# A hybrid decoder layer on one core: the down projection with VectorE and ScalarE in a hand-written issue order

## The chip, the core and the metric

The kernel runs on one core of a Trainium2 chip. The metric is the device time of one execution in microseconds (us). A step below is one product of one pair of feature chunks: 12 matmuls on TensorE (PE in the profile). VectorE is DVE there, ScalarE is ACT, GpSimd is POOL and SyncE is SP.

## What is computed

One layer over 1024 tokens of width 1024, all in float32: three mixers (pooling, sliding-window attention, spatial gating), then a gated convolution feed-forward network, whose second half is what the change is about:

```python
h = rms_norm(x, norm2[l])
up = causal_dwconv(h @ w_up[l], conv_w[l], conv_b[l])
gate, val = jnp.split(up, 2, axis=-1)
x = x + (jax.nn.silu(gate) * val) @ w_down[l]
```

The last line is the down stage. It contracts over 2816 features (22 chunks of 128) and adds its result to `out`, which holds the residual already.

## The kernel before, in words

Every float32 product is made from three matmuls: an operand is split into `hi` (ScalarE, line 86, a rounding copy) and `lo` (VectorE, line 87, the operand less `hi`), and hi·hi, hi·lo and lo·hi are added up in PSUM.

**The down stage** (from line 981) is one round of Strassen's method in Winograd's form. The 22 chunks make 11 pairs `q`; a pair's tile `raws[q]` has eight 128x512 blocks, A11 to A22 of the activations (`gd`, spilled to DRAM by the up stage) and B11 to B22 of `w_down`. From them come seven products, P1 to P7, and each product is accumulated in four PSUM banks over the pairs of a part. There are two parts, pairs 0 to 5 and 6 to 10, so 7 x 11 = 77 steps. `ORDERS` says in which order the products come: P1, P2, P6, P7, P4, P3, P5 in the first part, P5 ahead of P3 in the second. P1 and P2 share four banks, P6, P7 and P4 share four, P3 and P5 share four; a product that continues in banks of another one needs the other one read out first.

- `operands` makes the operands of one step: for P7 and P4 first a subtraction on VectorE (lines 1024 and 1029), then `split`. It is called three steps ahead (`ahead = 3`). `hi` has four buffers ("w") and `lo` has four ("x"), so the operands of step j+3 get theirs only when TensorE is done with step j-1.
- `presum` makes two sums for a pair (lines 1009 and 1010, VectorE), which P6, P5 and P4 use. It is called in the steps of P2.
- `evacuate` reads a product's banks after its last step: with ScalarE for P1 (line 1052) and P2 (line 1055), with VectorE for P6 and P7 (line 1058), P4 (line 1060), P3 (line 1064), P5 (line 1050) and the last result (line 1076). Results go to `out` by accumulating DMAs that POOL issues (`add`, line 1041). In the second part `olds` reads one quarter of `out` into SBUF, VectorE adds to it, and SP writes it with a plain DMA (line 1077).
- `fetch` loads a part's blocks with DMAs on SP (line 997): the halves for P1 and P2 of all pairs, then the other halves. The second part's `fetch` stands behind the first step of P3; its tiles use the buffers of the first part's (two "hh", five "hq", one of the five being the tile `sv` that keeps P1).
- `gate` (lines 879 to 885) is the last work of the up stage on a chunk: two convolutions (a ScalarE activation, line 871, and two VectorE operations, line 875, each), a Silu (line 883), a product (line 884) and the spill to `gd`. `conv` takes its output tile from the four "x" buffers too. At the end of the up stage the generators that are left run out, the last of them (chunk 21) behind `fetch`.

The program's text doesn't set the order on an engine: the framework's planner orders the instructions of each engine by a simulated timeline, so in the kernel before VectorE takes, for example, subtractions of P7 and P4 long before their steps. The four "raw" tiles of P2 (`raw`, three buffers) go out by DMA before a buffer is taken again.

Of the kernel before, what the change touches and what calls it, by code (L numbers as in the profile page):

```python
# [38 lines left out]
def trunk_kernel(tc, x, positions, norm1, w_in, q_norm, k_norm, sinks, w_pool, pool_scale,  # L39
                 sgu_v_norm, w_s, b_s, w_proj_a, w_proj_b, w_proj_c, w_out, norm2,  # L40
                 w_up, conv_w, conv_b, w_down, cst_d, out, dbg=None, stop=None):
    nc = tc.nc
    act, dve, pe, pool, sp = nc.scalar, nc.vector, nc.tensor, nc.gpsimd, nc.sync
    x, out = x[0], out[0]
# [34 lines left out]
    def sm2(n=T, dt=F32):  # L79
        return slot("sm2", 5, [P, n], dt)  # L80
# [35 lines left out]
    for dst, src in ((0, norm1), (8, norm2), (16, pool_scale)):  # L116
        n = src.shape[1] // P
# [92 lines left out]
    def new_h():  # L210
        return [t[:, k] for t in [slot("hh", 2, [P, HK, 2, T], F32R) for _ in range(2)] for k in range(HK)]
# [7 lines left out]
    h = new_h()  # L219
# [423 lines left out]
    st = Stream(w_in, 768, 256, KD, normed.ins)  # L643
    for t in range(2):
        kv = t4([P, NT, 256])
        qs = [t4([P, 2, T]) for _ in range(2)]
        st = tok_major(h, st, lambda i, ps: act.activation(kv[:, i, :], ps, AF.Copy), (w_in, 256, T, KD))
# [4 lines left out]
        st = tok_major(h, st, lambda i, ps: act.activation(qs[i // 2][:, i % 2, :], ps, AF.Copy), (w_in, 1024, T, KD))  # L652
# [9 lines left out]
        u, v = t4([P, NT, 256]), t4([P, NT, 256])  # L662
# [13 lines left out]
        part = slot("part", 1, [P, KD, T], F32)  # L676
# [34 lines left out]
        for i, c0 in enumerate(units):  # L711
            if i + 1 < len(units):
                wn = w_gran(w_in, units[i + 1])
            else:
                x2t = [slot("x2" if t == 0 else "x", 4, [P, D], F32) for _ in range(NT)]
                for b in range(NT):
                    r = t * T + b * P
                    sp.dma_start(x2t[b], x[r : r + P, :])
                st = Stream(w_out, 0, T, KD)
            if i >= 2:  # L720
                kind, n = ((i - 2) % 2, (i - 2) // 2) if i < 18 else (2, i - 18)
# [10 lines left out]
            ps = mm_ps()  # L732
# [15 lines left out]
        if t == 0:  # L748
            h = new_h()
# [6 lines left out]
        for nh in range(2):  # L756
# [6 lines left out]
            ahead = (w_out, T, T, KD) if nh == 0 else (w_in, 768, 256, KD) if t == 0 else None  # L763
            st = tok_major(merged, st, evo, ahead)
# [122 lines left out]
    gates = []  # L887
# [58 lines left out]
    while full:  # L946
        late = [(rest[0], n, REST) for n in REST] if rest and len(full) <= 2 * len(rest) else []
# [36 lines left out]
    raws, sums, ops = {}, {}, {}  # L984

    def two(r, a, b):
        return r[:, a : b + 1 : b - a, :]
# [11 lines left out]
    def fetch(a, b):  # L999
        for j, q in enumerate(range(a, b)):  # L1000
            raws[q] = slot("hh", 2, [P, 8, T], F32) if j in (0, 2) else h_([P, 8, T])
            sums[q] = {}
            load(q, (A11, B11, A12, B21))
        for q in range(a, b):
            load(q, (A21, B12, A22, B22))

    def presum(r, st):
        st["1"], st["2"] = q_([P, 2, T]), q_([P, 2, T])
        dve.tensor_tensor(st["1"], two(r, A21, B12), two(r, A22, B11), ALU.add)
        dve.tensor_tensor(st["2"], st["1"], two(r, A11, B22), ALU.subtract)  # L1010

    def operands(p, r, st):

        if p == "P1":
            src = two(r, A11, B11)
        elif p == "P6":
            src = st["2"]
        elif p == "P2":  # L1020
            src = two(r, A12, B21)
        elif p == "P7":
            src = two(r, A11, B12)
            dve.tensor_tensor(src, src, two(r, A21, B22), ALU.subtract)
        elif p == "P5":
            src = st["1"]
        elif p == "P4":
            d4 = two(r, A12, B21)
            dve.tensor_tensor(d4, d4, st["2"], ALU.subtract)
            src = two(r, A22, B21)  # L1030
        else:
            src = two(r, A12, B22)
# [4 lines left out]
    state = {}  # L1037

    def add(i, dh, o):

        pool.dma_start(out[i * P : (i + 1) * P, dh * T : (dh + 1) * T], o, accum_op=ALU.add)

    def evacuate(part, p, i, ps):


        if p == "P1" and i == 0:
            state["sv"] = h_([P, 8, T])
            state["v3"] = [sm2() for _ in range(NT)]
        s, v2, v3 = state["sv"][:, i, :], state["sv"][:, NT + i, :], state["v3"][i]
        over = lambda v: dve.scalar_tensor_tensor(v, v, -1.0, ps, ALU.mult, ALU.add)  # L1050
        if p == "P1":
            act.activation(s, ps, AF.Copy)
        elif p == "P2":
            o = raw([P, T])
            act.activation(o, ps, AF.Copy)
            add(i, 0, o)
        elif p in ("P6", "P7"):
            dve.tensor_tensor(v2 if p == "P6" else v3, s, ps, ALU.add)
        elif p == "P4":
            dve.tensor_tensor(s, s, ps, ALU.add)  # L1060
            add(NT + i, 0, s)
        elif part + 1 < len(parts):
            if p == "P3":
                dve.tensor_tensor(v3, v3, ps, ALU.add)  # L1064
            else:
                for ti, v in ((i, v2), (NT + i, v3)):
                    over(v)
                    add(ti, 1, v)
        elif p == "P5":
            over(v3)  # L1070
            add(NT + i, 1, v3)
            o = state["o"][:, i, :]
            dve.tensor_tensor(o, o, v2, ALU.subtract)
        else:
            o = state["o"][:, i, :]
            dve.tensor_tensor(o, o, ps, ALU.add)
            sp.dma_start(out[i * P : (i + 1) * P, T:], o)

    def olds():

        state["o"] = h_([P, NT, T])
        for i in range(NT):
            sp.dma_start(state["o"][:, i, :], out[i * P : (i + 1) * P, T:])

    todo = [(part, p, q) for part, (a, b) in enumerate(parts) for p in ORDERS[part] for q in range(a, b)]
    ahead = 3
    for g in gates[:-1]:
        for _ in g:
            pass
    fetch(*parts[0])  # L1090
    for g in gates[-1:]:
        for _ in g:
            pass
    for j in range(ahead):
        _, p, q = todo[j]
        ops[todo[j]] = operands(p, raws[q], sums[q])
    sets = {}
    for j, (part, p, q) in enumerate(todo):
        a, b = parts[part]
        start = q == a and p in ("P1", "P6", ORDERS[part][-2])  # L1100
        if start:
            sets[p] = [bank() for _ in range(NT)]
        ps = sets["P1" if p in ("P1", "P2") else "P6" if p in ("P6", "P7", "P4") else ORDERS[part][-2]]
        if p == "P2":
            presum(raws[q], sums[q])
        if p == "P4" and q == a and part + 1 == len(parts):
            olds()
# [63 lines left out]
```

## Time and profile before

| what | us |
|---|---|
| median of 3 runs (1332.35 to 1333.76) | 1332.39 |
| the profiled execution, its own time | 1330.77 |
| its span, from the first to the last instruction | 1329.0 |
| TensorE busy | 1290.5 (97%) |
| VectorE busy | 968.4 (73%) |
| ScalarE busy | 603.7 (45%) |

The span is cut from the hardware profiler's record of one execution. 1.77 us of that execution lie outside the span. Busy TensorE includes the run of a matmul through the array, so that 0.39 us of busy time stand for a new matmul every 0.227 us; lost time is therefore read from the starts of matmuls, not from the busy share.

### The profile page before, as it was taken

The numbers are of one execution on the slowest core, as the hardware profiler recorded it, in microseconds if no ns is written. First come the engines' busy times: TensorE is split into PE (matmuls) and PEld (weight loads), VectorE is DVE, ScalarE is ACT, GpSimd is POOL, SyncE is SP. The second block draws the span as 40 slices with busy tenths as digits, with TensorE's granted clock in tenths as the row PEclk, the third lists the DMA queues.
The fourth block names the chain that finished last, engine by engine and source line by source line (L and its number), as shares of the span: only waits on it lengthen the run. The fifth ranks groups of instructions, "written<-read, shape, count | busy, mean of one in ns | idle before, by whom it ended". The sixth has DMA issues, their size and how long they took to land.

```text
span 1329.0 us, 16065 instructions
## 1 busy us (share of the span) xinstructions
PE 1290.5 (97%) x5956; PEld 1065.6 (80%) x5956; DVE 968.4 (73%) x1516; ACT 603.7 (45%) x982; POOL 192.1 (14%) x123
## 2 busy tenths in 40 slices
PE   6999999999999999999999999999999998999998
PEld 6888888888888888888877877878878776787787
DVE  6887865544579676456575899889989979757865
ACT  5655554333465554333573434434444443433432
POOL 0000000000000000000005444444244400100302
PEclk9999999999999999999999999999999998999999
DMA  6422224322432222543554323323333174236705
GB/s 232 123 83 62 80 80 150 112 72 95 155 107 64 80 79 79 155 120 113 200 176 132 111 73 111 102 80 111 111 96 111 64 250 177 32 113 236 117 11 95
DMA packets 167644, 151.25 MB, mean 114 GB/s; under 512 B 7615, under 2 KB 132493, under 8 KB 167565
## 3 DMA queue, kind: packets, MB, share of 16 engines
q1 hardware_dynamic: 163533, 142.87, 33.8%
q0 software_dynamic: 4032, 7.34, 3.8%
q8 instruction: 47, 0.77, 0.2%
q14 instruction: 32, 0.26, 0.1%
HBM read 120.30 MB, written 29.88 MB: 113 GB/s over the span
## 4 chain that ended last, share of the span: by engine, by line
issue 53%; DVE 17%; PE 15%; DMA 6%; ACT 4%; POOL 1%; SPq 0%; DVEq 0%; ACTq 0%; POOLq 0%
DVE x L875 6%; PE bk L1115 4%; PE bk L1116 4%; PE bk L1114 4%; DMA raw<-in_w_up_dram 3%; DVE q L87 3%; ACT x L871 2%; DVE x L87 2%; PE bk L898 2%; PE bk L900 2%; PE bk L899 2%; DVE w L87 1%; DMA hh<-gd 1%; ACT w L86 1%; ACT x L883 1%
## 5 line engine op out<-in xcount | busy, mean ns | idle before, releaser
L173 PE MATMUL mm<-hh,w 128*128 128x512 f32 x416 | 162.6, 391 | 0.0
L175 PE MATMUL mm<-hh,w 128*128 128x512 f32 x416 | 162.5, 391 | 0.0
L174 PE MATMUL mm<-hh,w 128*128 128x512 f32 x416 | 162.4, 390 | 0.0
L858 POOL TENSOR_TENSOR q<-raw 128x512 f32<-128x512 f32 x22 | 38.3, 1740 | 841.9 <-DVE w L87 651.3
L87 DVE TENSOR_TENSOR w<-raw,w 128x1024 fp32r<-128x1024 f32 (+1 forms) x96 | 93.3, 976 | 86.3 <-ACT w L86 86.3
L86 ACT ACTIVATE w<-raw 128x1024 fp32r<-128x1024 f32 (+1 forms) x96 | 82.3, 858 | 153.2 <-PE mm L174 67.1
L875 DVE SCALAR_TENSOR_TENSOR x<-q,cA,x 128x1023 f32<-128x1023 f32 (+1 forms) x88 | 134.5, 1534 | 22.7 <-ACT x L871 22.2
L898 PE MATMUL bk<-hq,q 128*128 128x512 f32 x352 | 139.1, 395 | 5.4 <-DVE sm L916 4.6
L899 PE MATMUL bk<-hq,q 128*128 128x512 f32 x352 | 137.6, 391 | 0.0
L900 PE MATMUL bk<-hq,q 128*128 128x512 f32 x352 | 137.4, 391 | 0.0
L1115 PE MATMUL bk<-x,w 128*128 128x512 f32 x308 | 122.9, 399 | 7.8 <-DVE x L87 7.8
L1116 PE MATMUL bk<-w,x 128*128 128x512 f32 x308 | 121.9, 396 | 0.0
L1114 PE MATMUL bk<-w 128*128 128x512 f32 x308 | 102.8, 399 | 4.2 <-DVE sm L1064 3.0
L174 PEld LDWEIGHTS mm<-hh,w 128*128 128x128 f32 x416 | 78.1, 188 | 16.1
L175 PEld LDWEIGHTS mm<-hh,w 128*128 128x128 f32 x416 | 78.1, 188 | 15.9
L173 PEld LDWEIGHTS mm<-hh,w 128*128 128x128 f32 x416 | 78.1, 188 | 15.8
L87 DVE TENSOR_TENSOR wa<-raw,wa 128x512 fp32r<-128x512 f32 x72 | 49.4, 694 | 55.7 <-ACT wa L86 55.7
L898 PEld LDWEIGHTS bk<-hq,q 128*128 128x128 f32 x352 | 66.5, 189 | 24.5 <-DVE sm L916 7.1
L871 ACT ACTIVATE x<-q,cA 128x1024 f32<-128x1024 f32 x44 | 54.0, 1240 | 65.5 <-DVE q L926 35.6
L86 ACT ACTIVATE wa<-raw 128x512 fp32r<-128x512 f32 x72 | 45.1, 631 | 79.5 <-PE mm L175 67.4
L1115 PEld LDWEIGHTS bk<-x,w 128*128 128x128 f32 x308 | 59.2, 192 | 23.3 <-DVE x L87 11.1
L900 PEld LDWEIGHTS bk<-hq,q 128*128 128x128 f32 x352 | 66.4, 189 | 14.1
(267 smaller groups left out, 2956.9 us busy)
## 6 DMA issues: line engine op xcount, KB each, us to landing
raw<-in_w_in_dram SPq DMA_DIRECT2D x72, 512.0 KB, 3.8
raw<-in_w_up_dram SPq DMA_DIRECT2D x51, 512.0 KB, 4.6
gd<-x SPq DMA_DIRECT2D x22, 512.0 KB, 2.8
x<-in_x_dram SPq DMA_DIRECT2D x16, 512.0 KB, 4.1
raw<-in_w_out_dram SPq DMA_DIRECT2D x16, 512.0 KB, 3.6
hq<-gd SPq DMA_DIRECT2D x28, 256.0 KB, 5.3
hq<-in_w_down_dram SPq DMA_DIRECT2D x28, 256.0 KB, 5.8
raw<-in_w_proj_b_dram SPq DMA_DIRECT2D x32, 128.0 KB, 2.8
```

The source lines that it names most:

```text
L86: split.last = act.activation(hi, src, AF.Copy).ins
L87: dve.tensor_tensor(lo, src, f(hi), ALU.subtract)
L173: pe.matmul(ps, a(0), b(0), start=first, stop=False)
L174: pe.matmul(ps, a(0), b(1), start=False, stop=False)
L175: r = pe.matmul(ps, a(1), b(0), start=False, stop=last)
L875: dve.scalar_tensor_tensor(y[:, n:], u[:, 0 : S - n], col(w), y[:, n:], ALU.mult, ALU.add)
L898: pe.matmul(ps, ws[n][:, 0, k, :], rhs[n](0, k), start=start and k == 0, stop=False, skip_group_check=True)
L899: pe.matmul(ps, ws[n][:, 0, k, :], rhs[n](1, k), start=False, stop=False, skip_group_check=True)
L900: pe.matmul(ps, ws[n][:, 1, k, :], rhs[n](0, k), start=False, stop=k == HK - 1, skip_group_check=True)
L1114: pe.matmul(ps[i], hi[:, 0, ts], hi[:, 1, :], start=start, stop=False, skip_group_check=True)
L1115: pe.matmul(ps[i], hi[:, 0, ts], lo[:, 1, :], start=False, stop=False, skip_group_check=True)
L1116: pe.matmul(ps[i], lo[:, 0, ts], hi[:, 1, :], start=False, stop=q == b - 1, skip_group_check=True)
```

## The change

VectorE and ScalarE run the down stage in the order of the program's text (`tc.manual_schedule`); TensorE, POOL and SP stay with the planner. The products come as P1, P2, P6, P3, P7, P5, P4 in both parts; the subtraction that belonged to P4 moves to P3. The last gate is no longer emitted as a whole ahead of the steps: one piece of its generator is taken at the start of each of the first eight steps. `presum` is called where the table `SUMS` says. An `evacuate` is emitted one step late, behind the next `operands`, except for P1's and that of the last product. P3 gets a copy of its own in SBUF (`p3`, ScalarE), which VectorE adds to `v3` after P7. In the second part P5 now goes out by eight accumulating DMAs, and the quarter that is read back and written by SP is the one of P4. The second `fetch` stands behind the first step of P4 and `olds` behind the first of P7. The set of banks is named "P3" where it was named by `ORDERS[part][-2]`.

```diff
-    ORDERS = (("P1", "P2", "P6", "P7", "P4", "P3", "P5"), ("P1", "P2", "P6", "P7", "P4", "P5", "P3"))
+    ORDER = ("P1", "P2", "P6", "P3", "P7", "P5", "P4")
+    SUMS = {("P1", 4): 0, ("P1", 5): 1, ("P2", 1): 2, ("P2", 2): 3, ("P2", 4): 4, ("P2", 5): 5}, \
+           {("P1", 3): 0, ("P1", 4): 1, ("P2", 1): 2, ("P2", 2): 3, ("P2", 4): 4}
...
+    def operands(p, q):
...
+        elif p == "P3":
+            d4 = two(r, A12, B21)
+            dve.tensor_tensor(d4, d4, sums[q][1], ALU.subtract)
+            src = two(r, A12, B22)
         elif p == "P7":
             src = two(r, A11, B12)
             dve.tensor_tensor(src, src, two(r, A21, B22), ALU.subtract)
         elif p == "P5":
-            src = st["1"]
-        elif p == "P4":
-            d4 = two(r, A12, B21)
-            dve.tensor_tensor(d4, d4, st["2"], ALU.subtract)
+            src = sums[q][0]
+        else:
             src = two(r, A22, B21)
...
         hi, lo = slot("w", 4, [P, 2, T], F32R), slot("x", 4, [P, 2, T], F32R)
         split(hi, lo, src)
...
+        elif p == "P6":
+            dve.tensor_tensor(v2, s, ps, ALU.add)
+        elif p == "P3":
+            act.activation(p3, ps, AF.Copy)
+        elif p == "P7":
+            v3 = state["v3"][i] = sm2()
+            dve.tensor_tensor(v3, s, ps, ALU.add)
+            dve.tensor_tensor(v3, v3, p3, ALU.add)
+        elif p == "P5":
+            for ti, v in ((i, v2), (NT + i, v3)):
+                over(v)
+                add(ti, 1, v)
+            if part + 1 == len(parts):
+                o = state["o"][:, i, :]
+                dve.tensor_tensor(o, o, s, ALU.add)
+        elif part + 1 < len(parts):
             dve.tensor_tensor(s, s, ps, ALU.add)
             add(NT + i, 0, s)
...
         else:
             o = state["o"][:, i, :]
             dve.tensor_tensor(o, o, ps, ALU.add)
-            sp.dma_start(out[i * P : (i + 1) * P, T:], o)
+            sp.dma_start(out[(NT + i) * P : (NT + i + 1) * P, 0:T], o)
...
     fetch(*parts[0])
-    for g in gates[-1:]:
-        for _ in g:
-            pass
+    own = tc.manual_schedule(engines={mybir.EngineType.DVE, mybir.EngineType.Activation})
+    own.__enter__()
     for j in range(ahead):
-        _, p, q = todo[j]
-        ops[todo[j]] = operands(p, raws[q], sums[q])
-    sets = {}
+        ops[todo[j]] = operands(*todo[j][1:])
+    sets, late = {}, []
...
+        if j < 8:
+            next(gates[-1], None)
+        ps = sets["P1" if p in ("P1", "P2") else "P6" if p in ("P6", "P7", "P4") else "P3"]
         if j + ahead < len(todo):
-            pn, n, qn = todo[j + ahead]
-            ops[todo[j + ahead]] = operands(n, raws[qn], sums[qn])
+            ops[todo[j + ahead]] = operands(*todo[j + ahead][1:])
+        if (p, q - a) in SUMS[part]:
+            presum(a + SUMS[part][p, q - a])
+        for args in late:
+            evacuate(*args)
+        late = []
...
             if q == b - 1:
-                evacuate(part, p, i, ps[i])
-        if p == "P3" and q == a and part + 1 < len(parts):
-            fetch(*parts[part + 1])
+                if p in ("P1", "P4") and part + 1 == len(parts) or p == "P1":
+                    evacuate(part, p, i, ps[i])
+                else:
+                    late.append((part, p, i, ps[i]))
+        if p == "P4" and q == a:
+            if part + 1 < len(parts):
+                fetch(*parts[part + 1])
+        if p == "P7" and q == a and part + 1 == len(parts):
+            olds()
+    own.__exit__(None, None, None)
```

## Rows read from the trace of the kernel before

**Rows 1.** Busy time by stretch; the last three columns are granted clock, DMA share, GB/s

```profile
1094.00:1323.00 229.00, 217.00 (x917) 175.07 (x916) 169.60 (x168) 87.28 (x92) 24.85 (x28) 0.97 0.44 113
1098.00:1104.00 6.00, 5.62 (x14) 4.43 (x15) 6.00 (x6) 1.06 (x1) 0.00 (x0) 0.53 1.05 378
1106.00:1121.00 15.00, 13.55 (x55) 9.59 (x54) 15.00 (x14) 7.89 (x10) 0.00 (x0) 1.00 0.40 152
```

**Rows 2.** Groups of instructions, TensorE, one of the down stage's three matmul lines

```profile
L1115 PE MATMUL bk<-x,w 128*128 128x512 f32 x308 | 122.9, 399 | 7.8 <-DVE x L87 7.8
```

**Rows 3.** Timeline of TensorE in the down stage: start, duration, idle time before and its releaser

```profile
1098.38 0.80 PE L1115 MATMUL bk<-x,w 128*128 128x512 f32 x1 [4.01 <-DVE x L87]
...
1109.97 0.50 PE L1115 MATMUL bk<-x,w 128*128 128x512 f32 x1 [0.68 <-DVE x L87]
...
1123.04 0.39 PE L1115 MATMUL bk<-x,w 128*128 128x512 f32 x1
1123.27 0.39 PE L1116 MATMUL bk<-w,x 128*128 128x512 f32 x1
...
1153.30 0.47 PE L1114 MATMUL bk<-w 128*128 128x512 f32 x1 [0.38 <-DVE hq L1058]
...
1206.22 0.77 PE L1114 MATMUL bk<-w 128*128 128x512 f32 x1 [3.02 <-DVE sm L1064]
...
1235.64 0.50 PE L1115 MATMUL bk<-x,w 128*128 128x512 f32 x1 [2.23 <-DVE x L87]
```

**Rows 4.** Timeline of VectorE in the down stage

```profile
1097.11 1.22 DVE L87 TENSOR_TENSOR x<-hh,w 128x1024 fp32r<-128x1024 f32 x1
...
1151.33 1.23 DVE L87 TENSOR_TENSOR x<-hh,w 128x1024 fp32r<-128x1024 f32 x1 [1.49 <-ACT w L86]
...
1186.44 2.47 DVE L1060 TENSOR_TENSOR hq<-hq,bk 128x512 f32<-128x512 f32 x4
...
1323.00 2.48 DVE L1076 TENSOR_TENSOR hq<-hq,bk 128x512 f32<-128x512 f32 x4 [3.12 <-PE bk L1116]
```

**Rows 5.** Waits of the down stage: total us, times, longest

```profile
ACT w L86 <- PE bk L1116: 119.2, 51, 10.6
...
DVE q L1009 <- DMA hh<-gd: 6.4, 2, 6.2
```

**Rows 6.** Timeline of ScalarE in the down stage

```profile
1150.24 1.06 ACT L86 ACTIVATE w<-hh 128x1024 fp32r<-128x1024 f32 x1 [1.66 <-PE bk L1116]
...
1187.15 1.06 ACT L86 ACTIVATE w<-hq 128x1024 fp32r<-128x1024 f32 x1 [1.89 <-DVE hq L1060]
...
1254.82 1.57 ACT L1055 ACTIVATE raw<-bk 128x512 f32<-128x512 f32 x3 [0.75 <-PE bk L1116]
...
1259.72 0.60 ACT L1055 ACTIVATE raw<-bk 128x512 f32<-128x512 f32 x1 [2.38 <-DMA out_dram<-raw]
```

**Rows 7.** Groups of instructions, VectorE, 1096 to 1323 us: count, busy, mean ns

```profile
L1010 DVE TENSOR_TENSOR q<-q,hq 128x1024 f32<-128x1024 f32 x7 | 8.5, 1220 | 0.9 <-DMA hq<-in_w_down_dram 0.9
...
L875 DVE SCALAR_TENSOR_TENSOR x<-q,cA,x 128x1023 f32<-128x1023 f32 (+1 forms) x4 | 5.1, 1279 | 0.0
```

**Rows 8.** Timeline of POOL: first and last of the first part's eight adds of P5

```profile
1229.54 0.88 POOL L1041 DMA_DIRECT2D out_dram<-hq  x1 [32.18 <-DVE hq L1050]
...
1241.03 0.87 POOL L1041 DMA_DIRECT2D out_dram<-sm  x1 [0.94 <-DVE x L87]
```

**Rows 9.** DMA issues, median us to landing: 1225 to 1245 us, 1180 to 1220 us

```profile
out_dram<-sm POOLq DMA_DIRECT2D x4, 256.0 KB, 5.1
...
out_dram<-hq POOLq DMA_DIRECT2D x4, 256.0 KB, 9.2
```

**Rows 10.** Timeline of the SP queue: first and last load of part two, last writes

```profile
1181.79 0.33 SPq L997 DMA_DIRECT2D hh<-gd  x1
...
1213.60 0.33 SPq L997 DMA_DIRECT2D hq<-in_w_down_dram  x1
...
1323.71 2.12 SPq L1077 DMA_DIRECT2D out_dram<-hq  x4
```

More of the change, by code (lines that the diff above doesn't have):

```diff
@@ L982, in trunk_kernel @@
     parts = ((0, 6), (6, 11))
-    ORDERS = (("P1", "P2", "P6", "P7", "P4", "P3", "P5"), ("P1", "P2", "P6", "P7", "P4", "P5", "P3"))
-    raws, sums, ops = {}, {}, {}
+    ORDER = ("P1", "P2", "P6", "P3", "P7", "P5", "P4")
+    SUMS = {("P1", 4): 0, ("P1", 5): 1, ("P2", 1): 2, ("P2", 2): 3, ("P2", 4): 4, ("P2", 5): 5}, \
+           {("P1", 3): 0, ("P1", 4): 1, ("P2", 1): 2, ("P2", 2): 3, ("P2", 4): 4}
+    raws, sums, ops, states = {}, {}, {}, [{}, {}]
     def two(r, a, b):
@@ L1005, in fetch, with presum @@
             load(q, (A21, B12, A22, B22))
[L1007 to L1012, printed above, removed]
+    def presum(q):
+        r = raws[q]
+        sums[q] = s1, s2 = q_([P, 2, T]), q_([P, 2, T])
+        dve.tensor_tensor(s1, two(r, A21, B12), two(r, A22, B11), ALU.add)
+        dve.tensor_tensor(s2, s1, two(r, A11, B22), ALU.subtract)
+    def operands(p, q):
+        r = raws[q]
         if p == "P1":
             src = two(r, A11, B11)
-        elif p == "P6":
-            src = st["2"]
         elif p == "P2":
             src = two(r, A12, B21)
+        elif p == "P6":
+            src = sums[q][1]
+        elif p == "P3":
+            d4 = two(r, A12, B21)
+            dve.tensor_tensor(d4, d4, sums[q][1], ALU.subtract)
+            src = two(r, A12, B22)
         elif p == "P7":
@@ L1025, in operands @@
         elif p == "P5":
-            src = st["1"]
-        elif p == "P4":
-            d4 = two(r, A12, B21)
-            dve.tensor_tensor(d4, d4, st["2"], ALU.subtract)
+            src = sums[q][0]
+        else:
             src = two(r, A22, B21)
-        else:
-            src = two(r, A12, B22)
         hi, lo = slot("w", 4, [P, 2, T], F32R), slot("x", 4, [P, 2, T], F32R)
@@ L1035, in operands @@
         return hi, lo
-    state = {}
     def add(i, dh, o):
@@ L1043, in evacuate @@
     def evacuate(part, p, i, ps):
[L1046 to L1049, printed above, removed]
+        state = states[part]
+        s, v2, v3, p3 = (state[n][i] for n in ("s", "v2", "v3", "p3"))
         over = lambda v: dve.scalar_tensor_tensor(v, v, -1.0, ps, ALU.mult, ALU.add)
@@ L1056, in evacuate @@
             add(i, 0, o)
-        elif p in ("P6", "P7"):
-            dve.tensor_tensor(v2 if p == "P6" else v3, s, ps, ALU.add)
-        elif p == "P4":
+        elif p == "P6":
+            dve.tensor_tensor(v2, s, ps, ALU.add)
[13 more added lines that the diff above has]
+        elif part + 1 < len(parts):
             dve.tensor_tensor(s, s, ps, ALU.add)
             add(NT + i, 0, s)
[L1062 to L1073, printed above, removed]
         else:
@@ L1076, in evacuate @@
             dve.tensor_tensor(o, o, ps, ALU.add)
-            sp.dma_start(out[i * P : (i + 1) * P, T:], o)
+            sp.dma_start(out[(NT + i) * P : (NT + i + 1) * P, 0:T], o)
     def olds():
-        state["o"] = h_([P, NT, T])
+        o = states[-1]["o"] = h_([P, NT, T])
         for i in range(NT):
-            sp.dma_start(state["o"][:, i, :], out[i * P : (i + 1) * P, T:])
-    todo = [(part, p, q) for part, (a, b) in enumerate(parts) for p in ORDERS[part] for q in range(a, b)]
-    ahead = 3
+            sp.dma_start(o[:, i, :], out[(NT + i) * P : (NT + i + 1) * P, 0:T])
     for g in gates[:-1]:
@@ L1089, in trunk_kernel @@
             pass
+    todo = [(part, p, q) for part, (a, b) in enumerate(parts) for p in ORDER for q in range(a, b)]
+    ahead = 3
     fetch(*parts[0])
-    for g in gates[-1:]:
-        for _ in g:
-            pass
+    own = tc.manual_schedule(engines={mybir.EngineType.DVE, mybir.EngineType.Activation})
+    own.__enter__()
     for j in range(ahead):
-        _, p, q = todo[j]
-        ops[todo[j]] = operands(p, raws[q], sums[q])
-    sets = {}
+        ops[todo[j]] = operands(*todo[j][1:])
+    sets, late = {}, []
     for j, (part, p, q) in enumerate(todo):
         a, b = parts[part]
-        start = q == a and p in ("P1", "P6", ORDERS[part][-2])
+        start = q == a and p in ("P1", "P6", "P3")
         if start:
             sets[p] = [bank() for _ in range(NT)]
[L1103 to L1107, printed above, removed]
-        if j + ahead < len(todo):
-            pn, n, qn = todo[j + ahead]
-            ops[todo[j + ahead]] = operands(n, raws[qn], sums[qn])
+            if p == "P1":
+                sv = h_([P, 8, T])
+                state = states[part]
+                state["s"], state["v2"] = ([sv[:, h * NT + i, :] for i in range(NT)] for h in range(2))
+                state["v3"], state["p3"] = [None] * NT, [None] * NT
+            elif p == "P3":
+                states[part]["p3"] = [t[:, h, :] for t in (q_([P, 2, T]) for _ in range(2)) for h in range(2)]
+        if j < 8:
+            next(gates[-1], None)
+        ps = sets["P1" if p in ("P1", "P2") else "P6" if p in ("P6", "P7", "P4") else "P3"]
+        if j + ahead < len(todo):
+            ops[todo[j + ahead]] = operands(*todo[j + ahead][1:])
[4 more added lines that the diff above has]
+        late = []
         hi, lo = ops.pop((part, p, q))
```

1 line of the change is left out of this document (removed).

## The prediction

> **What bounds the kernel now.** I first read the busy time by stretch. The down stage runs from 1094.0 us, where the last matmul of the up stage has started, to 1323.0, and the span ends 6.0 later [rows 1]. Then the groups of instructions: three lines of 308 matmuls, 924 = 77 steps of 12 [rows 2]. The timeline of TensorE gives their pace: starts at 1123.04 and 1123.27 are 0.227 us apart, so a step takes 2.72 us and 924 matmuls 209.7 [rows 3]. Four of them run before 1094.0 (0.9). The stage thus loses 229.0 - 208.8 = 20.2 us, and nothing else is there to win: where nothing is late, TensorE is the bound.
>
> The same timeline shows where the loss lies [rows 3]. At 1098.38 TensorE has stood 4.01 us for the first `lo`. Behind that, from 1098 to 1104, the granted clock is 0.53, mostly the lower of its two levels (1.2 instead of 2.4 GHz) [rows 1], and matmuls take about twice their time: some 2.4 us more. So the border costs 6.5. Steps 4 to 15 lose 3.3 in short gaps (0.68 at 1109.97) while VectorE is 15.00 of 15 us busy [rows 1, 3]. The entry into P7 at 1153.30, and two like it, lose 0.5 each: the banks must be read out first. The entry into P5 at 1206.22 loses 3.02, with the clock behind it 4.7: the read-out stands on VectorE behind a presum that waits for a load, 6.4 us in two waits [rows 3, 5]. At 1235.64 2.23 are lost, with the clock 3.8: eight read-outs stand ahead of a `lo` [rows 3]. Sum: 6.5 + 3.3 + 1.6 + 4.7 + 3.8 = 19.9 of 20.2; the other 0.3 are small.
>
> How operands are made matters for all that follows. A `lo` that starts at 1097.11 lets TensorE go on at 1098.38, 1.27 later; a `lo` takes 1.22, and the next VectorE operation can start 1.14 after it did [rows 3, 4]. The `hi` ahead of it takes 1.06: from 1150.24, then `lo` at 1151.33 [rows 4, 6]. ScalarE waits 119.2 us in 51 waits for TensorE: a `hi` can't start until a buffer is free [rows 5]. So `lo` of step j+3 ends at best 2.3 us into step j. It is due 8.2 us into it (three steps), and 0.9 later where the four hi·hi go first: a lead of 5.9 to 6.8.
>
> **The change, part by part.** *Taken away.* `operands` of the first three steps no longer stand behind the last gate for an "x" buffer, so the 6.5 at the border go. With P3 between P6 and P7, and P7 between P3 and P5, a read-out has a whole product of time (16 us) for 2.5 us of work (four in 2.47 [rows 4]): 1.6 and 4.7 go. Late read-outs behind the next operands take the 3.8. The 3.3 of the first steps go too, and are counted anew below. In all -19.9.
>
> *First steps.* The gate's two outputs hold two of four "x" buffers until its product, so around step 6 the lead is short. From the start of step 6 VectorE has, in the text's order: `lo` 7, presum, convolution, `lo` 8, presum, product, `lo` 9. A presum is two operations of 1.22 [rows 7], a convolution 1.28 [rows 7]: 3 x 1.14 + 2 x 2.4 + 1.28 + 1.22 = 10.7 us. `lo` 9 is due 8.2 + 0.9 = 9.1 later: +1.6. From there to `lo` 15 VectorE has six `lo` and four presums, 16.4 us in 16.3: the lead stays at nothing.
>
> *P3 and P7, the main term.* In the text's order each of their operands is subtraction, `hi`, `lo`, and each waits for the one before. The next subtraction stands behind this `lo` on VectorE and can't fill the wait. One operand costs 1.22 + 0.03 + 1.06 + 0.03 + 1.14 = 3.5 us against 2.72 of TensorE, 0.8 too much. The step from VectorE to ScalarE shows as 0.03 at 1187.15, where the first of four read-outs from 1186.44 has taken 0.68 [rows 4, 6]. The planner's order hid this, since it took those subtractions long before. In the first part there are 12 such operands in a row and P6's read-out (2.4) among them: 12 x 0.8 + 2.4 = 12.0. The two plain operands ahead (`lo` 16 and 17) bring a lead of 2 x 1.6 = 3.2, so 8.8 are lost. In the second part it is 10 x 0.8 + 2.4 = 10.4. There the lead would be full, but for P2's copies on ScalarE: the fourth starts 4.9 us after the first, as it waits for its buffer's DMA (1254.82 to 1259.72 [rows 6]). The `hi` of step 56 stands behind it and starts 1.1 + 4.9 + 0.6 = 6.6 us into step 52, its `lo` ends at 8.9 and is due at 11.8: a lead of 2.9, so 7.5 are lost. Bounds: with a full lead of 5.9 in both parts (12.0 + 10.4) - 11.8 = 10.6, with none 22.4. I take 16.3, the one that follows the queues.
>
> *Costs nothing:* P3's copies (four on ScalarE, which is 87.28 of 229 us busy [rows 1]) and the four more additions per part on VectorE after P7: in P5's steps VectorE has 1.14 of 2.72 to do. If that cover went they would be 2.4 us a part. The entry from P1 to P2 stays.
>
> *The tail.* The last part's P5 now sends eight adds instead of four. The first starts about 3.4 us into step 72. The eight of the first part took 1229.54 to 1241.03, and 5.1 more to land [rows 8, 9]: 16.6, so the last lands at 20.0, where TensorE ends at 13.6 (five steps): 6.4 behind it. The four last writes are issued over 2.12 us in that time [rows 10] and share the DMA engines: 8.5. Today the span ends 6.0 behind TensorE [rows 1]. So +2.5. Bounds: +0.4 if the adds lose nothing to the writes, +4.5 if they land as slowly as under loads (9.2 [rows 9]).
>
> *Sum.* TensorE: -19.9 + 1.6 + 8.8 + 7.5 = -2.0; tail +2.5; together +0.5 on the profiled execution's 1330.77 (span 1329.0 and 1.8 around it): 1331.3. The median of the runs is 1.6 above that execution, so 1332.9.
>
> **Rivals.** *Full lead (1325.6).* If the queues don't eat the lead, the main term is 10.6 instead of 16.3 and the first steps cost nothing: 1332.9 - 5.7 - 1.6. For it: both losses of lead hang on an order I worked out by hand. Against: VectorE was full in these very steps [rows 1].
>
> *A load that comes late for the queue in order (1339.1).* The blocks of the second part get their buffers only as P4's operands are made, so loading begins at step 33 to 34 and has 22 us until P1; before it began at 1181.79, 33 us ahead. It takes 32 us of issue (to 1213.60 [rows 10]). P5's eight adds now fall into it. If a presum of P1 or P2 stands and waits for a block, `lo` stands behind it, and a wait as long as before's longest (6.2 [rows 5]) takes the lead and goes straight to TensorE: 1332.9 + 6.2. It decides once the loads end later than about 46 us after their start, where the last presum stands. Today's 32 and 6 to land leave 8.
>
> *The clock.* From 1106 to 1121 TensorE stands 0.4 to 0.7 us every 3.4 us, and the granted clock stays 1.00, the upper level [rows 1, 3]. P3 and P7 would have gaps of 0.8 in 3.5. If the clock fell there, a step would take 5.4 instead of 3.5, in some 17 steps: +33, about 1366. The Trainium skill (TensorE: Matmul & The Clock Gate, A second HAM failure mode: psum-queue depth-cycling) says that frequent small idle times between groups of matmuls can make the clock swing between its levels. By that rule this change would be much slower; the trace so far doesn't bear it out.
>
> *The order isn't kept (1316.6).* If the planner still takes the subtractions early, the 16.3 go.
>
> **How the numbers follow.** Forecast 0.52, with a range of its own from 1329 to 1337; full lead 0.21; late load 0.17; clock 0.04; order not kept 0.06. A measurement of this kernel can tell some 0.2%, 2.7 us, from no change. Of the forecast I put 0.08 of its share below 1329.7 and 0.25 above 1335.1. Faster: 0.21 + 0.06 + 0.04 = 0.31. Slower: 0.17 + 0.04 + 0.13 = 0.34. Same: 0.35. The range reaches to both neighbours, 1325.5 to 1339.5, and leaves out the clock and the unkept order.
>
> **What would show it.** Right: TensorE goes from line 900 to the down stage without a gap; in P3 and P7 matmul groups start 3.5 us apart, and VectorE's `lo` waits some 1.1 us for ScalarE each time, behind its own subtraction; P6's and P7's read-outs hold nothing; the last add lands behind the last write. Wrong: steps of 2.72 in P7, a wait of `lo` for a DMA, a granted clock of 0.5 in P7, or a gap at the border.

## The result, and the profile after

The changed kernel takes 1353.50 us (median of 6 runs, 1350.55 to 1355.18) against 1332.28 for the one before (6 runs beside them). The ratio is 1.016, its 95% interval 1.0142 to 1.0178. The forecast was 1332.9, and its range ended at 1339.5: the change is slower, by 21 us. The profiled execution of after took 1350.55 (span 1348.8), 19.8 more than the one profiled before.

Lines have moved: the three matmul lines are 1121 to 1123, the loads 999, presums 1011 and 1012, the subtraction of P3 1027, that of P7 1031, the adds 1042.

First the time by stretch [rows 1]: the whole stage, three places in it, and what follows TensorE's last matmul.

```profile
1101.00:1338.30 237.30, 218.27 (x898) 169.71 (x897) 175.32 (x174) 90.33 (x101) 22.48 (x26) 0.96 0.36 97
1108.00:1120.00 12.00, 9.15 (x32) 6.45 (x31) 7.27 (x7) 6.96 (x9) 0.00 (x0) 0.86 0.41 153
1162.00:1190.00 28.00, 23.99 (x86) 16.17 (x86) 18.14 (x17) 10.64 (x13) 0.00 (x0) 0.94 0.00 1
1236.00:1250.00 14.00, 7.03 (x25) 5.36 (x24) 6.61 (x6) 6.99 (x9) 1.80 (x3) 0.76 1.08 322
1338.35:1348.80 10.45, 0.39 (x2) 0.00 (x0) 1.52 (x3) 0.00 (x0) 2.18 (x3) 0.67 0.87 198
```

The last matmul of the up stage starts at 1101.35, the last of all at 1338.35. Of the down stage's 924 matmuls 29 ran ahead of 1101.35 (4 in before), which leaves 895 of 0.2268 us in 237.0 us: 34.0 us are lost. The same count for before gives 21.3. Behind the last matmul's start come 10.45 us, where before has 5.07:

```profile
1323.93:1329.00 5.07, 0.39 (x2) 0.00 (x0) 1.55 (x3) 0.00 (x0) 0.00 (x0) 0.99 0.56 207
```

What lies ahead of the stage adds 1.7: the up stage ends 7.4 later, but TensorE has run 25 matmuls (5.7) of the down stage more by then. So 1.7 + 12.7 + 5.4 = 19.8.

The timeline of TensorE [rows 3] shows where the 34.0 are, and its group line [rows 2] what they wait for: ScalarE's `hi`, 18.1 us, where before it was VectorE's `lo`.

```profile
L1121 PE MATMUL bk<-w 128*128 128x512 f32 x297 | 90.6, 407 | 18.1 <-ACT w L86 18.1
```

```profile
1111.56 1.21 PE L1121 MATMUL bk<-w 128*128 128x512 f32 x4 [2.80 <-ACT w L86]
...
1126.43 1.19 PE L1121 MATMUL bk<-w 128*128 128x512 f32 x4 [0.75 <-ACT w L86]
...
1164.70 2.08 PE L1121 MATMUL bk<-w 128*128 128x512 f32 x4 [2.61 <-ACT w L86]
...
1171.89 1.20 PE L1121 MATMUL bk<-w 128*128 128x512 f32 x4
...
1175.45 1.20 PE L1121 MATMUL bk<-w 128*128 128x512 f32 x4 [0.20 <-ACT w L86]
...
1243.38 2.07 PE L1121 MATMUL bk<-w 128*128 128x512 f32 x4 [6.97 <-ACT w L86]
...
1290.33 1.72 PE L1121 MATMUL bk<-w 128*128 128x512 f32 x4 [2.63 <-ACT w L86]
```

Added up from the starts of matmuls, each place with the half clock behind its gap:

| place | foreseen us | measured us |
|---|---|---|
| step 5 (1111.56) | 0 | 5.1 |
| first steps (1126.43 and 1135.20) | 1.6 | 1.7 |
| P3 and P7, first part (1162 to 1192) | 8.8 | 9.0 |
| step 46, P1 of pair 10 (1243.38) | 0 | 8.7 |
| P3 and P7, second part (1280 to 1310) | 7.5 | 9.1 |
| small gaps | 0.3 | 0.4 |
| behind the last matmul, against before | +2.5 | +5.4 |

**P3 and P7.** Steps start 3.56 us apart (1171.89, 1175.45). VectorE and ScalarE [rows 4, 6] show why: subtraction, `hi`, `lo`, next subtraction, each behind the one before it.

```profile
1169.44 1.22 DVE L1031 TENSOR_TENSOR hh<-hh 128x1024 f32<-128x1024 f32 x1
1171.87 1.23 DVE L87 TENSOR_TENSOR x<-hh,w 128x1024 fp32r<-128x1024 f32 x1 [1.21 <-ACT w L86]
1173.01 1.22 DVE L1031 TENSOR_TENSOR hq<-hq 128x1024 f32<-128x1024 f32 x1
...
1243.36 1.23 DVE L87 TENSOR_TENSOR x<-hq,w 128x1024 fp32r<-128x1024 f32 x1 [12.18 <-ACT w L86]
```

```profile
1110.45 1.06 ACT L86 ACTIVATE w<-hq 128x1024 fp32r<-128x1024 f32 x1 [7.53 <-DMA hq<-in_w_down_dram]
...
1170.77 1.06 ACT L86 ACTIVATE w<-hh 128x1024 fp32r<-128x1024 f32 x1 [2.51 <-DVE hh L1031]
...
1242.27 1.06 ACT L86 ACTIVATE w<-hq 128x1024 fp32r<-128x1024 f32 x1 [14.74 <-DMA hq<-in_w_down_dram]
```

**Two late loads.** The first and the last of these ScalarE rows are the other large losses. A `hi` waits for its pair's load, and everything on ScalarE and VectorE stands behind it, since their order is fixed: VectorE's `lo` waits 12.18 us. The waits of the stage [rows 5] have the two loads in one line. The presums, which waited 6.4 us for loads before, now wait 0.2 (VectorE's groups, [rows 7]).

```profile
DVE x L87 <- ACT w L86: 59.3, 35, 12.2
...
ACT w L86 <- DMA hq<-in_w_down_dram: 22.3, 2, 14.7
```

```profile
L1012 DVE TENSOR_TENSOR q<-q,hq 128x1024 f32<-128x1024 f32 x7 | 8.6, 1225 | 0.2
```

SP's queue [rows 10], first in before and then in after. The one row of before is pair 5's first load; the rows of after are pair 5's first load, the first load of part two, pair 10's B11, the last load, the last writes.

```profile
1096.61 0.33 SPq L997 DMA_DIRECT2D hq<-gd  x1
```

```profile
1104.38 0.33 SPq L999 DMA_DIRECT2D hq<-gd  x1
...
1204.88 0.33 SPq L999 DMA_DIRECT2D hh<-gd  x1
...
1231.21 0.33 SPq L999 DMA_DIRECT2D hq<-in_w_down_dram  x1
...
1246.62 0.33 SPq L999 DMA_DIRECT2D hq<-in_w_down_dram  x1
...
1338.11 2.12 SPq L1077 DMA_DIRECT2D out_dram<-hq  x4
```

Pair 10's B11 is issued 26.3 us after the loading began and lands 10.9 us later (1242.1); step 46 could have begun at 1236.25. Issue of part two's loads takes 41.7 us, where before it took 31.8. Much of this is waiting: from 1204 to 1248 us SP stands 25.6 us, in 28 waits, for the landing of earlier loads. Meanwhile POOL [rows 8] sends P5's eight adds, and P4's four behind them; the last two rows are the first and the last add of the tail.

```profile
1213.42 0.87 POOL L1042 DMA_DIRECT2D out_dram<-hq  x1 [70.85 <-DVE hq L1049]
...
1229.86 0.88 POOL L1042 DMA_DIRECT2D out_dram<-sm  x1 [1.17 <-DVE hq L1072]
...
1329.25 0.86 POOL L1042 DMA_DIRECT2D out_dram<-hq  x1 [59.17 <-DVE hq L1049]
...
1340.71 0.87 POOL L1042 DMA_DIRECT2D out_dram<-sm  x1 [0.63 <-issue]
```

The DMA queues and issues from 1200 to 1245 us [rows 9]: loads are q1, adds q0.

```profile
q1 hardware_dynamic: 4661, 8.51, 54.7%
q0 software_dynamic: 1633, 2.98, 35.9%
...
hq<-in_w_down_dram SPq DMA_DIRECT2D x11, 256.0 KB, 9.0
...
out_dram<-hq POOLq DMA_DIRECT2D x8, 256.0 KB, 6.8
```

### The profile page after: what moved, and what is told of

Read it like the earlier page. It is cut to its first block, busy times and chain, and to the rows that moved or that the text cites. A ratio compares the mean times of both kernels' runs of the same rounds, so it can differ in the third digit from the quotient of the medians.

```text
span 1348.8 us, 16081 instructions
## 1 busy us (share of the span) xinstructions
PE 1298.2 (96%) x5956; PEld 1066.3 (79%) x5956; DVE 973.1 (72%) x1520; ACT 606.4 (45%) x990; POOL 191.8 (14%) x123
## 5 line engine op out<-in xcount | busy, mean ns | idle before, releaser
L875 DVE SCALAR_TENSOR_TENSOR x<-q,cA,x 128x1023 f32<-128x1023 f32 x88 | 134.4, 1533 | 23.0 <-ACT x L871 22.4
L1121 PE MATMUL bk<-w 128*128 128x512 f32 x308 | 94.1, 406 | 18.1 <-ACT w L86 18.1
L1121 PEld LDWEIGHTS bk<-w 128*128 128x128 f32 x308 | 57.6, 192 | 37.0 <-ACT w L86 25.4
```

What stands on the lines that cost most here:

```text
L875: dve.scalar_tensor_tensor(y[:, n:], u[:, 0 : S - n], col(w), y[:, n:], ALU.mult, ALU.add)
```

## The experiments

Each edit is against the changed kernel; "after" is its 1353.5. All medians stand beside runs of the kernel before on the same chip, 1331.8 to 1331.9, and 1330.1 for the last three variants.

**Subtractions one step ahead.** They are taken out of `operands`.

```diff
+    def before(p, q):
+        r = raws[q]
+        if p == "P3":
+            d4 = two(r, A12, B21)
+            dve.tensor_tensor(d4, d4, sums[q][1], ALU.subtract)
+        elif p == "P7":
+            d7 = two(r, A11, B12)
+            dve.tensor_tensor(d7, d7, two(r, A21, B22), ALU.subtract)
...
             presum(a + SUMS[part][p, q - a])
+        if j + ahead + 1 < len(todo):
+            before(*todo[j + ahead + 1][1:])
```

> The subtractions of P3 and P7 are issued one step ahead: behind the lo of step j+3 stands the subtraction of step j+4, so that it lies beside the hi on ScalarE. Theory (the three operations of one operand, VectorE, ScalarE, VectorE, wait for each other in turn, 3.57 us instead of 2.72): the gaps in P3 and P7 go, 8.8 us in the first part and 8.8 in the second, and the time falls by 15 to 18 us, to about 1336 to 1338; the stalls at step 5 (4.9) and at pair 10's P1 (8.7) stay or grow by some us, since the loads are not started earlier by as much as TensorE gains. Rival (VectorE is simply full in P3 and P7, or TensorE waits there for banks): the work of VectorE is the same, the step distance stays 3.5 and the time falls by less than 3 us.

Measured: 1349.68 (1.0132, interval 1.0107 to 1.0158). Neither side is tested, for the edit doesn't change what it was meant to. VectorE's timeline, then the `hi` that lies between its second and third row:

```profile
1167.64 1.23 DVE L87 TENSOR_TENSOR x<-hq,w 128x1024 fp32r<-128x1024 f32 x1 [1.26 <-ACT w L86]
1168.78 1.22 DVE L1021 TENSOR_TENSOR hh<-hh 128x1024 f32<-128x1024 f32 x1
1171.20 1.23 DVE L87 TENSOR_TENSOR x<-hh,w 128x1024 fp32r<-128x1024 f32 x1 [1.21 <-ACT w L86]
```

```profile
1170.11 1.06 ACT L86 ACTIVATE w<-hh 128x1024 fp32r<-128x1024 f32 x1 [2.51 <-DVE hh L1021]
```

`lo`, subtraction, `lo`: on an engine that runs in order the subtraction still stands directly ahead of its own `hi` and `lo`, one call earlier in the text and at the same place in the queue. The distance stays 3.56. The 3.8 us it gained are no more than single runs of after differ by (1350.55 to 1355.18), and the two intervals overlap; in its trace TensorE loses 35.6 us in the stage, not less than in after. The Trainium skill (TensorE: Matmul & The Clock Gate, the table at its head) says that VectorE's and ScalarE's queues are strictly first in, first out; these rows agree.

**Subtractions two steps ahead.** The same, but for one number.

```diff
-        if j + ahead + 1 < len(todo):
-            before(*todo[j + ahead + 1][1:])
+        if j + ahead + 2 < len(todo):
+            before(*todo[j + ahead + 2][1:])
```

> The subtractions of P3 and P7 are issued two steps ahead (of step j+5 between the lo of steps j+3 and j+4). One step ahead changed nothing in the order of VectorE: subtraction, lo, subtraction, lo stayed in a row, with each hi between a subtraction and its own lo. Two ahead, the hi of a step waits for a subtraction that ended before the lo ahead of it, and lies beside the next subtraction. Theory (chain of three in turn): VectorE's own work for an operand is 1.14 + 1.22 = 2.4 us, below 2.72; the step distance in P3 and P7 falls from 3.57 to 2.72, the 8.8 us of each part go but for what P6's read-out takes from the lead (0 to 2 each part), and the time falls by 14 to 17 us to about 1337 to 1339. Rival (VectorE is full, or ScalarE's hi is held by TensorE's buffers): step distance stays over 3.3 and the time falls by less than 4.

Measured: 1335.28 (10 runs; 1.0029, 1.0016 to 1.0042), 18.2 less than after and a little more than the 14 to 17 expected. VectorE's timeline and TensorE's two stretches of P3 and P7 by window:

```profile
1167.01 1.22 DVE L1021 TENSOR_TENSOR hh<-hh 128x1024 f32<-128x1024 f32 x1
1168.14 1.22 DVE L87 TENSOR_TENSOR x<-hq,w 128x1024 fp32r<-128x1024 f32 x1
1169.28 1.22 DVE L1021 TENSOR_TENSOR hq<-hq 128x1024 f32<-128x1024 f32 x1
1170.41 1.22 DVE L87 TENSOR_TENSOR x<-hh,w 128x1024 fp32r<-128x1024 f32 x1
```

```profile
1160.00:1200.00 40.00, 40.00 (x179) 33.11 (x178) 32.09 (x33) 16.97 (x19) 0.00 (x0) 1.00 0.05 14
1262.00:1300.00 38.00, 38.00 (x169) 31.47 (x168) 31.09 (x30) 18.02 (x20) 1.61 (x2) 1.00 0.18 27
```

Here no `lo` waits; one follows the other in 2.27 us, below TensorE's 2.72, and TensorE is busy throughout. With the same number of operations on every engine the whole of both chains is gone: the chain in turn is shown, a full VectorE is not the cause. Of the 18.1 us lost in P3 and P7 nothing is left in this trace; the two late loads cost more than in after's (6.4 us at step 5, 11.6 at pair 10), so TensorE loses 19.8 us in all.

**Blocks of the first part free six steps earlier.**

```diff
-    ORDER = ("P1", "P2", "P6", "P3", "P7", "P5", "P4")
+    ORDERS = ("P1", "P2", "P6", "P7", "P3", "P4", "P5"), ("P1", "P2", "P6", "P3", "P7", "P5", "P4")
...
+        elif p == "P3" and three_last:
+            dve.tensor_tensor(v3, v3, ps, ALU.add)
...
-                if p in ("P1", "P4") and part + 1 == len(parts) or p == "P1":
+                if p in ("P1", "P4") and part + 1 == len(parts) or p == "P1" or (part == 0 and p == "P6"):
```

> The first part takes its products in the order P1 P2 P6 P7 P3 P4 P5 instead of P1 P2 P6 P3 P7 P5 P4: the last use of the input blocks lies one product (six steps) earlier, so that the loads of the second part begin some 16 us earlier. The number of operations is the same. Theory (the 8.7 us at pair 10's P1 are a load that begins too late): that stall goes whole, the time falls by 8 to 9 us to about 1345, while the gaps of P3 and P7 (8.8 each part) and the 4.9 at step 5 stay. Rival (the load is slow because the adds of P5 share the DMA engines and the issue, whenever it begins): P5's adds now come last and fall beside P1 of the second part itself, the stall stays or moves to pairs 8 to 10, and the time moves by less than 3 us.

Measured: 1346.27 (1.0108, 1.0089 to 1.0127), 7.2 less. The stall at pair 10 is gone whole. But the order puts P7 directly behind P6 in the same banks, and TensorE waits for P6's read-out, which is emitted at once here and still stands on VectorE behind three operands of P7 in their chain (TensorE's timeline):

```profile
1156.95 0.76 PE L1125 MATMUL bk<-w 128*128 128x512 f32 x1 [6.07 <-DVE hq L1058]
```

So P3 between P6 and P7 does prevent a wait, as foreseen; in before, with the same order and no chain, this wait was 0.38 us [rows 3]. By the trace this entry costs 7.7 us; the operands gain a lead in the gap, so that the rest of the chain of this part loses 5.3 instead of 9.0; and the 8.7 at pair 10 are gone. With the small differences elsewhere TensorE loses 29.9 us instead of 34.0.

**SP's queue in the order of the text.**

```diff
-    own = tc.manual_schedule(engines={mybir.EngineType.DVE, mybir.EngineType.Activation})
+    own = tc.manual_schedule(engines={mybir.EngineType.DVE, mybir.EngineType.Activation, mybir.EngineType.SP})
```

> SyncE's queue too is kept in the order of the text from the down stage on: the first halves of all five pairs of the second part stand ahead of every second half (pair 10's first loads at place 354 of the queue instead of 364, ten loads of 256 KB earlier). Loads begin when they did. Theory (pair 10's hi waits for its load because seven loads that are needed later stand ahead of it): 7 to 10 loads of about 1 us of issue each lie behind it instead of ahead, so that all or nearly all of the 8.7 us at pair 10's P1 goes: time down by 6 to 9 us, to about 1346. Rival (loads are late because they begin late and share the DMA engines with the twelve adds of P5 and P4, whatever their order): the stall moves to pairs 8 and 9 or to the second halves (P2, presums) and at least 5 us of it stay.

Measured: 1342.39 as the median of three executions (a fourth, 5913.88, is out of line and left out, as in the ratio: 1.0083, 1.006 to 1.0106), 11.1 less where 6 to 9 were expected. ScalarE waits for no load from 1200 to 1260 us; pair 10's `hi` starts as soon as TensorE has freed its buffer:

```profile
1232.19 1.06 ACT L86 ACTIVATE w<-hq 128x1024 fp32r<-128x1024 f32 x1 [0.75 <-PE bk L1123]
```

The loads began no earlier against the stage: at 1208.79, 3.9 later than in after, where the up stage too ended 3.4 later (1104.75). Their order alone takes the stall away.

**Without the adds of P5 in the first part.**

```diff
-                add(ti, 1, v)
+                if part:
+                    add(ti, 1, v)
```

> Leaves out the eight accumulating DMAs of P5 in the first part (the right half of the output lacks what these rows of the first part add). Loads begin when they did and in the same order. Theory (late start and order in the queue, not contention, make the stall at pair 10's P1): some 2 to 4 us of the 8.7 go, as loads are issued 1 us apart or less once the adds don't share the DMA engines; at least 4 stay. Rival (contention with the adds): the whole stall goes, time down by 8 to 9 us to about 1345.

Measured: 1342.55 (1.008, 1.0063 to 1.0097), 11.0 less. ScalarE waits 1.5 us for pair 10's load and TensorE not at all; I had expected that at least 4 would stay. The queues from 1200 to 1245 us:

```profile
q1 hardware_dynamic: 6089, 11.10, 70.5%
q0 software_dynamic: 576, 1.05, 13.0%
```

In the same 45 us 11.10 MB go through the loads' queue (0.6 of them the reads of `olds`) instead of 8.51, and the 40 loads are issued in 27.6 us (1203.58 to 1231.19) instead of 41.7. The Trainium skill (DMA: Bandwidth & Descriptors, Issuing engines are not separate DMA queues) says that transfers run on the same 16 engines whichever engine starts them; adds that POOL issues and loads that SP issues do so here.

So none of the three is the cause by itself. TensorE stands 7.0 to 9.0 us for this load in the traces that have the stall, and an earlier begin, eleven loads less ahead of it, or eight adds less beside it each cover that. The stall differs from one execution to the next: it costs 8.7 us in after's trace (the profiled execution took 1350.55, the median 1353.50), and 11.0 and 11.3 in the traces of the next two variants, which change nothing around it. This fits the 11 us that two of the remedies brought.

**The up stage first.** TensorE's steps 0 to 2 stay behind the up stage's last matmul.

```diff
-            pe.matmul(ps[i], hi[:, 0, ts], hi[:, 1, :], start=start, stop=False, skip_group_check=True)
...
+            with tc.issue_after(up.last.ins) if j < 3 else nullcontext():
+                pe.matmul(ps[i], hi[:, 0, ts], hi[:, 1, :], start=start, stop=False, skip_group_check=True)
...
```

> TensorE's first three steps of the down stage are kept behind the last matmul of the up stage; nothing else is changed. Theory (the 4.9 us at step 5 are pair 5's hi, whose load waits for a buffer that the up stage frees late because 27 and more matmuls of the down stage run ahead of its last products): pair 5's first loads are issued 5 to 8 us earlier, the wait of 2.8 us and the half clock behind it go, and the time falls by 4 to 5 us to about 1349. Rival (the load is late since the issue on the SP queue is full at this place, whatever TensorE's order): the stall stays within 1 us of 2.9, and as the up stage's last read-outs now end ahead of nothing a gap at the border may open besides; time within 2 us of 1353.5.

Measured: 1351.14 (1.0143, 1.0124 to 1.0162), 2.4 less, and the two intervals overlap. The load of pair 5 goes out 6.3 us earlier (SP's queue) and the gap at step 5 is gone. But TensorE now stands within the up stage, with the half clock behind it, and this costs 4.3 (TensorE's timeline):

```profile
1098.11 0.32 SPq L999 DMA_DIRECT2D hq<-gd  x1
```

```profile
1091.90 0.79 PE L898 MATMUL bk<-hq,q 128*128 128x512 f32 x1 [2.51 <-DVE sm L919]
```

The gap is the up stage's own: line 919 is a read-out that stands on VectorE behind work of the last gates. With 29 matmuls put into it, as in the changed kernel, TensorE loses nothing there and 5.1 at step 5. Why the load is late there stays open in part. The edit moved two things: TensorE's order, and with it the planner's order of the loads, in which pair 5's first load is the 32nd of 48 instead of the 41st.

**Four adds in the tail.**

```diff
-                add(ti, 1, v)
+                if part == 0 or ti >= NT:
+                    add(ti, 1, v)
```

> Leaves out the second addition into the output of the last part's P5 (four of its eight accumulating DMAs, the quarter of the output with rows of the upper and columns of the right half lacks P5). Theory (the tail is set by eight adds through one queue, 1.6 us each): the span ends about 6 us behind the last matmul as before instead of 10.3, the time falls by 4 to 4.5 us to about 1349. Rival (the adds are held up by the four plain writes that share the DMA engines): the last add still lands 9 us or more behind the last matmul, and the time falls by 2 or less. TensorE's stalls are the same in both.

Measured: 1347.72 (1.0118, 1.0091 to 1.0145), 5.8 less. Behind the last matmul's start (by window):

```profile
1344.18:1349.90 5.72, 0.40 (x2) 0.00 (x0) 1.53 (x3) 0.00 (x0) 0.00 (x0) 0.96 0.60 203
```

5.72 instead of 10.45: the tail's surplus is the four adds more, 4.7 us. What the median gained beyond that is within the scatter of the runs (1344.68 to 1351.62). With them gone the four plain writes, issued until 1346, end last.

**All remedies.** Subtractions two ahead, SP's queue in the text's order, P4 ahead of P5 in the first part, and in the last part the upper right quarter of `out` read back, so that it leaves by plain writes. The first two edits stand above; P7 of the first part, which P4 now follows in the same banks, is read out at once; the others:

```diff
+    ORDERS = ("P1", "P2", "P6", "P3", "P7", "P4", "P5"), ("P1", "P2", "P6", "P3", "P7", "P5", "P4")
...
+            if part + 1 == len(parts):
+                dve.tensor_tensor(v2, v2, state["u"][i], ALU.subtract)
+            over(v2)
+            if part + 1 < len(parts):
+                add(i, 1, v2)
+            else:
+                sp.dma_start(out[i * P : (i + 1) * P, T : 2 * T], v2)
...
+        u = [t[:, h, :] for t in (q_([P, 2, T]) for _ in range(2)) for h in range(2)]
+        for i in range(NT):
+            sp.dma_start(u[i], out[i * P : (i + 1) * P, T : 2 * T])
```

> All remedies in one kernel: subtractions of P3 and P7 two steps ahead; SyncE's queue in the order of the text; the first part takes P4 ahead of P5, so that the second part's loads begin six steps (16 us) earlier; in the last part the upper right quarter of the output is read back and added on VectorE, so that P5 sends four adds instead of eight. Theory: of after's 1353.5 the two chains go (8.8 each, less 2), the stall at pair 10 (8.7) and 4 us of the tail: 1353.5 - 15.6 - 8.7 - 4 = about 1325, below the kernel before; the 4.9 at step 5 stays. Rival (VectorE, now with 4.9 us of subtractions more and the read-out of P7 directly ahead of P4, becomes the bound): TensorE waits for read-outs at the entry into P4 as much as the loads cost, time 1333 or more.

Measured: 1322.80 (0.9936, 0.9916 to 0.9955). The largest new gap is at the last `lo`, behind sixteen operations in a row, eight of read-out and eight additions that prepare read-outs (TensorE's timeline):

```profile
1310.66 0.50 PE L1140 MATMUL bk<-x,w 128*128 128x512 f32 x1 [2.77 <-DVE x L87]
```

**The same, with these eight additions spread over P5's steps, two in each.**

```diff
+        if part + 1 == len(parts) and p == "P5" and q > a:
+            st, i = states[part], q - a - 1
+            dve.tensor_tensor(st["v2"][i], st["v2"][i], st["u"][i], ALU.subtract)
+            dve.tensor_tensor(st["o"][:, i, :], st["o"][:, i, :], st["s"][i], ALU.add)
```

> As the kernel with all remedies, but the eight additions that prepare the last read-outs (old upper right quarter off v2, s onto the old lower left quarter) are spread over P5's steps, two in each, instead of standing among P5's read-outs. There sixteen VectorE operations in a row (1299.29 to 1309.46) held the last lo for 2.8 us. Theory: that gap goes, the last adds are issued some 5 us earlier in their row, time 1322.8 - 2.9 = about 1320, clearly below the kernel before. Rival (a lo in P5 gets late instead): time 1322 or more with new gaps at 1290 to 1300.

Measured: 1318.35 (1317.92 to 1321.31; 0.991, 0.9894 to 0.9927). The gap is gone. By window, the stage, step 5 and the tail:

```profile
1100.00:1311.60 211.60, 206.83 (x896) 169.65 (x895) 176.13 (x178) 90.57 (x100) 21.32 (x24) 0.98 0.44 116
1106.00:1116.00 10.00, 6.62 (x19) 4.93 (x18) 3.65 (x3) 6.40 (x8) 0.00 (x0) 0.70 0.60 223
1311.65:1319.50 7.85, 0.39 (x2) 0.00 (x0) 1.55 (x3) 0.00 (x0) 0.00 (x0) 0.70 0.75 204
```

TensorE loses 8.8 us instead of 34.0, 6.6 of it at step 5. This version beats both kernels: about 12 us below the one before, 35 below the changed one.

**Two variants of it.** The first also keeps TensorE's first steps behind the up stage, the second leaves the first part's P5 ahead of P4.

> As the one before, and TensorE's first three steps are kept behind the last matmul of the up stage. Theory (a gap at the border is exchanged: 5.0 us at step 5 against some 4.9 in the up stage where the read-outs of its gates set the pace): by itself this gave 2.4 us, so 1317 to 1320 here. Rival (pure exchange): within 1 us of the kernel without it.

> As the kernel with all remedies spread, but the first part keeps its order P5, P4, so loads begin six steps later and only the order of SyncE's queue helps them. Theory (either remedy alone is enough for pair 10, as with first halves first): no stall at P1 of the second part, time within 2 us of the kernel with both, about 1320. Rival (with the chains gone P1 comes 8.8 us earlier as measured from the first free buffer of the second part's loads, and the margin is lost): a stall of 2 us or more returns at P1.

Measured: 1318.60 (0.9914, 0.9898 to 0.993) and 1318.85 (0.9915, 0.9901 to 0.993), both within 1 us of it. So nothing clear of noise is won at the border (the two profiled executions lost 6.6 us at step 5 and 2.8 in the up stage, but with 1321.31 and 1316.46 us they lie at opposite ends of their runs), and the order of SP's queue is enough for pair 10.

## Why the prediction was wrong

**What held.** The main term: 8.8 and 7.5 us for P3 and P7, measured 9.0 and 9.1, from the chain that was worked out (3.5 us an operand; 3.56). That the lead is eaten in the second part was right but too kind by 1.6, in the main because the `lo` of step 56 (1269.79) ends 9.8 us into step 52 instead of 8.9, and an operand costs 0.84 too much instead of 0.8. The first steps cost 1.7 for 1.6, in part by luck: at 1126.43 TensorE waits for a `hi` that stands on ScalarE behind the gate's Silu, which the sum doesn't have. The gaps at the entries into P7 and P5 and of the eight read-outs are gone. The clock rival fell: from 1171.60 to 1191.60 TensorE lost 0.84 us by its starts in every 3.56, and the granted clock was 1.00, the upper level; in this stage it fell only behind the gaps of 2.6 us and more. The rule of the Trainium skill named there (TensorE: Matmul & The Clock Gate, A second HAM failure mode: psum-queue depth-cycling) didn't show in this kernel.

**The step that failed most: "Today's 32 and 6 to land leave 8", in the rival of the late load.** The rival was the right one and had 0.17. It was set aside because the last load would end 38 us after the loading began and the last presum stands 46 us after it. Two things were wrong with this. The critical load isn't the last one: pair 10's first half is due at step 46, 31 us after the loading begins, and 11 loads of second halves stood ahead of it in SP's queue. And the 32 us of issue were taken from a stretch without P5's adds; beside them it took 41.7, and the last load landed 47.1 us after the loading began (1251.98), behind the 46 that the rival itself set. The rival's price, 6.2, was before's longest wait of a presum; that 8.7 was measured, at a `hi` and not at a presum, is near by luck.

**"So the 6.5 at the border go."** They did at the border, but 5.1 came back at step 5. The step looked at VectorE's queue only. TensorE and SP stayed with the planner, which put 29 matmuls of the new stage into the up stage's gap, so that its last products ended 7.4 later, and put pair 5's first load at the 41st of 48 places in SP's queue, where before it had the 33rd. It went out at 1104.38 instead of 1096.61. TensorE's last product, which frees buffers for these loads, had ended at 1101.74, so at the end it was the queue that held the load. That the planner moved it because it foresaw the buffer late is likely, but not shown. Keeping the matmuls out removes the late load and brings back the gap, 4.3 for 5.1.

**The tail, +2.5, measured +5.4, above its bound of +4.5.** The adds took 11.46 us of issue, as the rows of before had it, and the last landed 7.0 after its issue, against 7.2 foreseen. Three smaller things were missed: the first add came 4.3 us into step 72 instead of 3.4; the span ends 1.2 behind the last landing; and before's own distance was read from 1323.0, where its last matmul starts at 1323.93, so it is nearer to 5 than to 6.

Against the forecast of 1331.3 for the profiled execution the 19.2 us more are these, within 0.1: 8.7 and 5.1 for the two loads, 2.9 of the tail, 2.0 of the two chains, the first steps and the small gaps, and 1.7 ahead of the stage, less 1.1 by which before's loss was read too low: its TensorE lost 21.3 where I had 20.2, mostly by the same early end at 1323.0. What lies ahead of the stage is nearly the same code. The end of the up stage, less the matmuls that had run ahead of it, lies at 1093.1 in before, at 1094.8 in after, and between 1092.1 and 1098.2 in the nine variants that don't tie TensorE's order, so the 1.7 is no more than scatter.

## What to carry to other kernels

When two engines pass one operand back and forth (subtract, round, subtract), a hand-written order must put the first operation two operands ahead of the last; one ahead leaves the queue as it was. A hand-written order of some engines leaves the others with the planner: go through their queues as well, TensorE's and the loads', and ask of every load when its own consumer wants it, not when the last one ends. Where the order is fixed, one late load stops both engines and then TensorE.

## What the runs showed that I had not expected

By the time that its packets took, an accumulating DMA beside loads occupies the DMA engines about 1.9 times as long per byte as a load: 35.9% for 2.98 MB against 54.7% for 8.51 (12.0 to 6.4% per MB), and 13.0% for 1.05 against 70.5% for 11.10 without P5's adds (12.4 to 6.3). In the tail, beside four plain writes, it was 2.4 times as long (1325 to 1349 us: 57.9% for 2.10 MB against 12.1% for 1.05). Eight adds of 256 KB beside the loads thus weigh, as an estimate from these shares, like fifteen loads. Three independent remedies each took away the whole of one stall, so "the cause" of a late load was no single one; a test that removes a stall shows a sufficient remedy only.
